# Both projections of a hybrid decoder layer as Strassen block products with seven instead of eight multiplications

## The chip, the cores and the metric

The kernel runs on one core of a Trainium2 chip. A core has TensorE (PE) for matmuls, whose results go to eight PSUM banks, VectorE (DVE), ScalarE (ACT) and GpSimd (POOL) for everything elementwise, and SyncE (SP), which here only issues DMAs. The metric is the time of one execution on the device, in microseconds (us); less is better. GpSimd has no access to PSUM.

## The reference

A sequence of 2048 tokens with 1024 channels is normalised, projected to 6144 columns, mixed by two groups of heads, normalised per head, gated, projected back, added to the input and normalised again. All in float32.

```python
xn = rms_norm(h, ln_g)                          # (2048, 1024)
proj = xn @ w_in                                # w_in (1024, 6144)
b_gate, c_gate, x_conv, g_conv, x_lru, g_lru = split(proj)      # six times 1024
y_conv = b_gate * conv3(c_gate * x_conv)                        # causal, per channel
y_conv = headwise_rms_norm(y_conv, 8, conv_out_g) * silu(g_conv)
u = conv4(x_lru) + lru_conv_b
r, i = sigmoid(u_head @ w_a + b_a), sigmoid(u_head @ w_i + b_i)  # 16 heads of 64
a = exp(8 * r * log_sigmoid(lam))
h_t = a_t * h_{t-1} + sqrt(1 - a_t**2) * (i_t * u_t)             # scan over tokens
y_lru = headwise_rms_norm(h_t, 16, lru_out_g) * silu(g_lru)
out = rms_norm(x + concat(y_conv, y_lru) @ w_out, final_g)      # w_out (2048, 1024)
```

## The kernel before

Channels lie on the partitions, 128 at a time, and tokens run along the free dimension. To keep float32 accuracy with the faster matmul format, every operand is split into a high part (rounded to that format) and a low part (the rest), and every product is three matmuls: high x high, high x low, low x high. A matmul here has a 128x128 stationary operand and a moving one of 128x512.

*Input projection.* The tokens are cut into four chunks of C = 512 (NC = 4). The normalised, transposed input of each chunk, xh[c] and xl[c], stays in SBUF. `load_w` (L215) loads one column tile of w_in (128 columns, all 1024 input channels), and GpSimd makes its two parts (L220, L221). `unit` (L224) multiplies one such tile with one chunk: 8 k tiles x 3 matmuls into one PSUM bank. The outer loop (L491) runs over steps of column tiles: "a" makes C and X and the short convolution (`conv_a`), "b" makes B and the gate G and finishes the conv head (`conv_b`), "l" makes an LRU tile and its gate (`lru`); the inner loop runs over the four chunks. `lru` computes the width-4 convolution u (L382, L385), stacks high and low halves of its two heads in stA and stB (L389, L390), and `lru_gates` multiplies them with the small gate matrices (L410). `lru_scan` does Tanh, Exp, Sqrt and the scan for two chunks at a time. `finish` (L265) applies gain and gate, spills the result to DRAM (yd) and prepares the squares whose sums over channels a matmul with a selector makes (L305); `head_norms` spills the reciprocal roots (rsd). `later` and `tick` put off matmuls that need such results by a few half steps.

*Output projection.* w_out is split and kept whole in SBUF (woh, wol). For each of 16 token blocks of 128, `load_z` (L459) loads the spilled rows and the head norms, multiplies them and splits; `out_mm` (L518) makes 2 x 16 x 3 matmuls into two banks; `epilogue` (L545) adds x, normalises and stores.

The tile framework schedules every engine's order by priority and readiness and inserts the semaphores.

Of the kernel before, what the change touches and what calls it, by code (L numbers as in the profile page):

```python
# [24 lines left out]
EPS = 1e-6  # L25

# columns of the packed per-channel parameters, eight per parameter row;
# b_i has its two heads swapped in each tile
# [3 lines left out]
# column groups of w_in, in tiles of 128  # L32
# [4 lines left out]
def hymba_kernel(ctx: ExitStack, tc: tile.TileContext, x, xt, w_in, par, lamc, w_gate, w_out, final_g, out):  # L37
# [3 lines left out]
    big = ctx.enter_context(tc.tile_pool(name="big", bufs=4))  # L41
    rawp = ctx.enter_context(tc.tile_pool(name="rawp", bufs=4))
    small = ctx.enter_context(tc.tile_pool(name="small", bufs=4))
    psu = ctx.enter_context(tc.tile_pool(name="psu", bufs=4, space=bass.MemoryType.PSUM))
    pss = ctx.enter_context(tc.tile_pool(name="pss", bufs=3, space=bass.MemoryType.PSUM))
# [4 lines left out]
    rsd = [dram.tile([NB, 3 * KT, P], F32, name=f"rsd{c}") for c in range(NC)]  # L50

    x0 = big.tile([P, NB, D], F32, tag="xl", name="x0")
    for b in range(NB):
        nc.sync.dma_start(x0[:, b, :], x[b * P:(b + 1) * P, :])
# [9 lines left out]
    # column P holds ones, columns 2P and 2P + KT ones for one 64-wide head each;  # L64
    # a sliding window puts them at any output row
    sel = const.tile([P, 3 * P], F32R, name="sel")
    nc.gpsimd.memset(sel.bitcast(F32), 0.0)
    nc.gpsimd.memset(sel.bitcast(F32)[:, P:P + 1], 1.0)
    nc.gpsimd.memset(sel.bitcast(F32)[:64, 2 * P:2 * P + 1], 1.0)
    nc.gpsimd.memset(sel.bitcast(F32)[64:, 2 * P + KT:2 * P + KT + 1], 1.0)  # L70
    ones = const.tile([P, P], F32R, name="ones")
    nc.gpsimd.memset(ones.bitcast(F32), 1.0)

    # 0 on the partitions of a head's high sums, -1 on those of the low ones
    lomask = const.tile([P, 1], F32, name="lomask")
    nc.vector.memset(lomask, 0.0)
    for p0 in (32, 96):
        nc.vector.memset(lomask[p0:p0 + 32, :], -1.0)

    # per-row divisor of the head sums: row 32c + j is head j of chunk c  # L80
    inv_hd = const.tile([P, 1], F32, name="inv_hd")
    nc.vector.memset(inv_hd, 1.0 / 64)
    for c in range(NC):
        nc.vector.memset(inv_hd[32 * c:32 * c + KT, :], 1.0 / 128)

    # klam = 8 * log_sigmoid(lam) = -8 * (relu(-lam) + log1p(exp(-|lam|)))
# [3 lines left out]
    def make_klam():  # L90
        lam = work.tile([P, 2, C], F32, tag="r", bufs=1, name="lam")[:, 0, 0:KT]
        nc.sync.dma_start(lam, lamc)
        w = [small.tile([P, KT], F32, tag=f"kl{j}", bufs=1, name="kl") for j in range(4)]
# [22 lines left out]
    xh = [None] * NC  # L116
    xl = [None] * NC
    norm_ps = psn.tile([P, C], F32, name="norm_ps")
    norm_first = [True]

    wp = ctx.enter_context(tc.tile_pool(name="wp", bufs=3))
    p1 = tc.tile_pool(name="p1", bufs=2)
    work = p1.__enter__()

    def wt(tag, name, bufs=2, dt=F32, n=C):
        return work.tile([P, n], dt, tag=tag, bufs=bufs, name=name)

# [5 lines left out]
    def alloc_xn(c):  # L133
        xh[c] = big.tile([P, KT, C], F32R, tag="xh", name=f"xh{c}")
        xl[c] = big.tile([P, KT, C], F32R, tag="xl", name=f"xl{c}")

    def prep_first():
        junk = big.tile([P, NB, D], F32, tag="xh", name="junk")
        for b in range(NB):
            ss = small.tile([P, 1], F32, tag="ss", name="ss")  # L140
            rs = small.tile([P, 1], F32, tag="rs", name="rs")
            nc.scalar.activation(out=junk[:, b, :], in_=x0[:, b, :], func=AF.Square, accum_out=ss)
            rstd(rs, ss)
            nc.vector.tensor_scalar(out=x0[:, b, :], in0=x0[:, b, :], scalar1=rs, scalar2=0.0,
                                    op0=ALU.mult, op1=ALU.add)
        alloc_xn(0)
        for k in range(KT):
            pool, tag = ((pss, "s"), (psu, "u"))[k % 2]
            tp = pool.tile([P, C], F32, tag=tag, name="tp")
            for b in range(NB):  # L150
                nc.tensor.transpose(tp[:, b * P:(b + 1) * P], x0[:, b, k * P:(k + 1) * P], ident)
            g = pt[:, LN_G + k:LN_G + k + 1]
            nc.scalar.activation(out=xh[0][:, k, :], in_=tp, func=AF.Copy, scale=g)
            nc.vector.scalar_tensor_tensor(out=xl[0][:, k, :], in0=tp, scalar=g,
                                           in1=xh[0][:, k, :].bitcast(F32),
                                           op0=ALU.mult, op1=ALU.subtract)
# [3 lines left out]
    def load_rows(c):  # L160
        rows = []
        early = big.tile([P, NB, D], F32, tag="xl", name="early") if c == 1 else None
        for b in range(NB):
            if c == 1:
                t = early[:, b, :]
            else:
                t = rawp.tile([P, D], F32, tag="raw", name="xrow")
            r0 = c * C + b * P
            nc.sync.dma_start(t, x[r0:r0 + P, :])
            rows.append(t)  # L170
        return rows

    def load_cols(c):
        cols = []
        cols4 = [work.tile([P, 2, C], F32, tag=tag, bufs=1, name="xcol2") for tag in ("r", "a", "T")]
        for k in range(KT):
            t = cols4[k // 2][:, k % 2, :] if k < 6 else wt("i", "xcol")
            nc.sync.dma_start(t, xt[k * P:(k + 1) * P, c * C:(c + 1) * C])
            cols.append(t)
        return cols  # L180

    def prep_sums(rows):
        ss = small.tile([P, NB], F32, tag="ss4", bufs=2, name="ss4")
        rs = small.tile([P, NB], F32, tag="rs4", bufs=2, name="rs4")
        for b in range(NB):
            nc.scalar.activation(out=rows[b], in_=rows[b], func=AF.Square, accum_out=ss[:, b:b + 1])
        rstd(rs, ss)
        rsh = small.tile([P, NB], F32R, tag="rsh", bufs=2, name="rsh")
        nc.vector.tensor_scalar(out=rsh, in0=rs, scalar1=1.0, scalar2=0.0, op0=ALU.mult, op1=ALU.add)
        nc.vector.tensor_tensor(out=rs, in0=rs, in1=rsh.bitcast(F32), op=ALU.subtract)  # L190
        dgh = wt("uh", "dgh", dt=F32R)
        dgl = wt("ul", "dgl", dt=F32R)
        for dg, part, eng in ((dgh, rsh.bitcast(F32), nc.vector), (dgl, rs, nc.gpsimd)):
            for b in range(NB):
                eng.tensor_scalar(out=dg[:, b * P:(b + 1) * P], in0=ident,
                                  scalar1=part[:, b:b + 1], scalar2=0.0,
                                  op0=ALU.mult, op1=ALU.add)
        return dgh, dgl

    def prep_chunk(c, dgs, cols):  # L200
        rb = pss.tile([P, C], F32, tag="s", name="rb")
        for n in range(2):
            nc.tensor.matmul(rb, ones, dgs[n], start=(n == 0), stop=(n == 1))
        alloc_xn(c)
        for k in range(KT):
            nc.vector.scalar_tensor_tensor(out=cols[k], in0=cols[k],
                                           scalar=pt[:, LN_G + k:LN_G + k + 1], in1=rb,
                                           op0=ALU.mult, op1=ALU.mult)
            nc.scalar.copy(xh[c][:, k, :], cols[k])
            eng = nc.gpsimd if k % 2 else nc.vector  # L210
            eng.tensor_tensor(out=xl[c][:, k, :], in0=cols[k],
                              in1=xh[c][:, k, :].bitcast(F32), op=ALU.subtract)

# [1 line left out]
    def load_w(j):  # L215
        raw = rawp.tile([P, D], F32, tag="raw", name="wraw")
        nc.sync.dma_start(raw, w_in[j])
        wh = wp.tile([P, D], F32R, tag="wh", name="wh")
        wl = wp.tile([P, D], F32R, tag="wl", name="wl")
        nc.gpsimd.tensor_scalar(out=wh, in0=raw, scalar1=1.0, scalar2=0.0, op0=ALU.mult, op1=ALU.add)  # L220
        nc.gpsimd.tensor_tensor(out=wl, in0=raw, in1=wh.bitcast(F32), op=ALU.subtract)  # L221
        return wh, wl
# [27 lines left out]
    def later(halves, f):  # L250
        queue.append([halves, f])
# [374 lines left out]
```

## Time and profile before

| | |
|---|---|
| time, median of 3 runs | 1579.53 us (1577.23 to 1580.32) |
| span of the profiled execution, first to last instruction | 1576.4 us |
| mean granted TensorE clock | 0.983 |
| matmuls | 6374 |
| busy: TensorE, VectorE, ScalarE, GpSimd | 96%, 49%, 35%, 23% |
| moved by DMA | 126.63 MB |

The profiled execution has no time of its own beside its span; the three runs are other executions of the same kernel. In the rows of the profile, a group of instructions is named by its line, engine, operation, written and read tiles, shapes and count; after the bar stand busy time (us), mean of one (ns) and the engine's idle time just before. A row of a window gives, after the length, the busy time and count of TensorE, its weight loads, VectorE, ScalarE and GpSimd, then the granted clock as a share, the busy share of the DMA engines and GB/s. In a timeline a row begins with start and duration in us.

### The profile page before, as it was taken

What the parts mean: (1) busy time and instruction counts of PE and PEld (TensorE: products, weight loads), DVE (VectorE), ACT (ScalarE), POOL (GpSimd) and SP (SyncE); (2) the same over time, 40 slices, a digit from 0 to 9 for tenths busy, and PEclk for the clock granted to TensorE, in tenths of its full rate; (3) what the DMA queues carried; (4) which work ended last, traced back from release to release, by engine and by line L of the source; (5) the groups of instructions that cost most, each with busy time, mean ns of one, the idle gap of its engine ahead of it and who ended that gap; (6) DMA issues with size and microseconds to landing.
All of it is one profiled execution on the core that took longest, in us unless ns stands there. A gap on an engine that the chain in (4) does not pass through costs nothing.

```text
span 1576.4 us, 16303 instructions
## 1 busy us (share of the span) xinstructions
PE 1510.8 (96%) x6374; PEld 1209.5 (77%) x6374; DVE 773.7 (49%) x927; ACT 558.0 (35%) x845; POOL 363.0 (23%) x267
## 2 busy tenths in 40 slices
PE   7999889998999899999989998999899999999998
PEld 6788677886888688778868886888687788888886
DVE  5765875257335633752464247325648533332331
ACT  6525554245226322542262236215336311111111
POOL 5531333203320322222232113320333100000000
PEclk9999999999999999999999999999999999999999
DMA  8420221012210211111121111110226754434420
GB/s 307 168 81 14 66 58 51 29 32 58 58 49 14 71 34 47 35 49 41 41 58 40 34 34 54 54 40 15 77 59 191 240 187 147 159 117 138 147 94 27
DMA packets 71289, 126.63 MB, mean 80 GB/s; under 512 B 7084, under 2 KB 41260, under 8 KB 71212
## 3 DMA queue, kind: packets, MB, share of 16 engines
q1 hardware_dynamic: 70924, 125.27, 25.4%
q8 instruction: 50, 0.82, 0.2%
q10 hardware_dynamic: 288, 0.32, 0.1%
q14 instruction: 27, 0.22, 0.0%
HBM read 91.81 MB, written 25.36 MB: 74 GB/s over the span
## 4 chain that ended last, share of the span: by engine, by line
PE 79%; DVE 9%; ACT 8%; issue 3%; DMA 1%; POOL 0%; SPq 0%; DVEq 0%; ACTq 0%; POOLq 0%
PE unit L232 54%; PE acc L524 22%; DVE u L433 2%; PE gate L410 2%; DVE u L385 1%; DVE a L435 1%; PE norm_ps L305 1%; ACT i L412 1%; ACT r L412 1%; DVE sg L266 1%; ACT L313 1%; ACT L427 1%; DVE u L414 1%; ACT stA L389 1%; DVE u L382 1%
## 5 line engine op out<-in xcount | busy, mean ns | idle before, releaser
L232 PE MATMUL unit<-xh,wh 128*128 128x512 f32 x1536 | 612.6, 399 | 0.0
L232 PE MATMUL unit<-xl,wh 128*128 128x512 f32 x1536 | 612.4, 399 | 0.0
L232 PE MATMUL unit<-xh,wl 128*128 128x512 f32 x1536 | 611.4, 398 | 0.0
L232 PEld LDWEIGHTS unit<-xh,wh 128*128 128x128 f32 x1536 | 292.0, 190 | 71.4
L232 PEld LDWEIGHTS unit<-xl,wh 128*128 128x128 f32 x1536 | 291.7, 190 | 71.2
L232 PEld LDWEIGHTS unit<-xh,wl 128*128 128x128 f32 x1536 | 291.5, 190 | 71.4
L524 PE MATMUL acc<-woh,zl 128*128 128x512 f32 x512 | 203.2, 397 | 2.2 <-DVE zl L473 2.2
L524 PE MATMUL acc<-woh,zh 128*128 128x512 f32 x512 | 203.0, 396 | 0.0
L524 PE MATMUL acc<-wol,zh 128*128 128x512 f32 x512 | 203.0, 396 | 0.0
L221 POOL TENSOR_TENSOR wl<-wraw,wh 128x1024 fp32r<-128x1024 f32 x48 | 120.2, 2504 | 3.8
L524 PEld LDWEIGHTS acc<-woh,zl 128*128 128x128 f32 x512 | 96.4, 188 | 26.5 <-DVE zl L473 3.1
L524 PEld LDWEIGHTS acc<-wol,zh 128*128 128x128 f32 x512 | 96.4, 188 | 23.5
L524 PEld LDWEIGHTS acc<-woh,zh 128*128 128x128 f32 x512 | 96.4, 188 | 23.4
L385 DVE SCALAR_TENSOR_TENSOR u<-xs,pt,u 128x512 f32<-128x512 f32 x96 | 96.3, 1003 | 2.7
L220 POOL TENSOR_SCALAR wh<-wraw 128x1024 fp32r<-128x1024 f32 x48 | 56.9, 1185 | 133.2 <-PE unit L232 125.6
L277 POOL TENSOR_TENSOR q<-q,q 64x512 f32<-64x512 f32 x32 | 42.7, 1335 | 170.0 <-ACT q L276 170.0
L473 DVE TENSOR_TENSOR zl<-zz,zh 128x1024 fp32r<-128x1024 f32 x32 | 41.8, 1305 | 76.2 <-ACT zh L472 76.2
L275 ACT ACTIVATE q<-t 64x512 f32<-64x512 f32 x32 | 20.2, 632 | 158.8 <-DVE t L352 149.7
L553 ACT ACTIVATE ob<-xr 128x512 f32<-128x512 f32 x32 | 20.1, 629 | 157.5 <-DVE xr L552 157.5
L472 ACT CAST zh<-zz 128x1024 fp32r<-128x1024 f32 x32 | 33.5, 1048 | 117.2 <-PE acc L524 108.6
L287 POOL TENSOR_TENSOR a<-a 128x512 f32<-128x512 f32 x32 | 41.0, 1301 | 146.9 <-DVE sg L266 142.5
L314 DVE TENSOR_TENSOR sg<-unit,sg 128x512 f32<-128x512 f32 x64 | 44.1, 689 | 60.6 <-ACT sg L313 60.6
(130 smaller groups left out, 1355.2 us busy)
## 6 DMA issues: line engine op xcount, KB each, us to landing
wraw<-in_w_in_dram SPq DMA_DIRECT2D x48, 512.0 KB, 3.5
yd<-sg SPq DMA_DIRECT2D x64, 256.0 KB, 2.3
zz<-yd SPq DMA_DIRECT2D x32, 512.0 KB, 4.1
qs<-a SPq DMA_DIRECT2D x128, 64.0 KB, 2.0
woraw<-in_w_out_dram SPq DMA_DIRECT2D x16, 512.0 KB, 3.8
zr<-rsd SPq DMA_DIRECT2D x32, 256.0 KB, 4.0
zr<-rsd SPq DMA_DIRECT2D x16, 512.0 KB, 5.9
xr<-in_x_dram SPq DMA_DIRECT2D x16, 512.0 KB, 5.8
```

Source lines behind the costliest of these rows:

```text
L220: nc.gpsimd.tensor_scalar(out=wh, in0=raw, scalar1=1.0, scalar2=0.0, op0=ALU.mult, op1=ALU.add)
L221: nc.gpsimd.tensor_tensor(out=wl, in0=raw, in1=wh.bitcast(F32), op=ALU.subtract)
L232: nc.tensor.matmul(ps, lhs, rhs, start=(n == 0), stop=(n == 3 * KT - 1))
L277: nc.gpsimd.tensor_tensor(out=q[lo], in0=q[lo], in1=q2[lo], op=ALU.add)
L287: nc.gpsimd.tensor_tensor(out=y, in0=y, in1=y, op=ALU.mult)
L314: nc.vector.tensor_tensor(out=sg, in0=gps, in1=sg, op=ALU.mult)
L385: nc.vector.scalar_tensor_tensor(out=u, in0=xs[:, j:j + C], scalar=lw[j], in1=u, op0=ALU.mult, op1=ALU.add)
L410: nc.tensor.matmul(ps, gw[n][:, j, :], st[j], start=(n == 0), stop=(n == 1))
L412: nc.scalar.activation(out=g[hi], in_=ps[src], func=AF.Sigmoid, bias=pt[src, bias + k:bias + k + 1])
L472: nc.scalar.copy(zh, zz)
L473: nc.vector.tensor_tensor(out=zl, in0=zz, in1=zh.bitcast(F32), op=ALU.subtract)
L524: nc.tensor.matmul(ps, lhs[:, k % KT, :], rhs[q][:, j, ds_], start=(k == KT and i == 0), stop=(k == KT - 1 and i == 2))
```

## The change

Every projection step becomes a 2x2 block product, [c11 c12; c21 c22] = A B, in the form of Strassen's scheme with seven multiplications and shared sums (Winograd's variant). A is the stationary side, B the moving one.

- *Input steps.* A step takes two column tiles (an "l", "a" or "b" pair, as before), so A's blocks are two tiles x two halves of the 1024 input channels, and B's are two channel halves x two chunks of 512 tokens. There are two passes over all 24 steps, one for each 1024 tokens (`h`); w_in is read in both. Of each block combination, `s_groups` makes the weight sums on VectorE and splits them (ScalarE the high parts; VectorE or GpSimd the low ones). `t_groups` does the same for the 7 x 4 moving tiles, which stay in SBUF for a whole pass.
- *Output steps.* The contraction over 2048 channels is cut into two passes (`ph`), first the LRU channels, then the conv ones. A step takes two token blocks as A and a set of w_out tiles as B. The first pass stores x plus its partial result to DRAM (od), the second adds it and normalises.
- A product is 4 k tiles x 3 matmuls, so a step has 84 matmuls instead of 96. Three products are accumulated on top of a bank that VectorE or ScalarE has read before; the other sums of products are made by VectorE from PSUM.
- TensorE's order is written out by hand (`tc.manual_schedule(engines={PE})`). A step has seven slots of one product. Slot by slot the weights of the next step are prepared, `load_next` loads two steps ahead, and elementwise work waits in `fifo`, from which each slot takes three items (`pop`). `later(n, f)` puts matmuls off by n slots. The first step after a change of B (steps 0, 24, 48, 56) runs over the k tiles on the outside instead, with seven banks open, while B's next tiles are being split.
- Elementwise work on a channel tile now takes 1024 tokens in one instruction; the conv and LRU states pass from the first half to the second through hx, hp and hl. Head sums take a high and a low part of the squares, two matmuls each for two chunks; the swaps of head halves by DMA are gone. The second half's normalised x^T is made during the first half (`second_sums`, `second_cols`) and stored in DRAM.

```diff
+    def s_groups(r, dst):                       # A: a11 a12 / a21 a22
+        a11, a12, a21, a22 = r
...
+        def g1():
+            t[1], t[2] = tmp(), tmp()
+            tt(t[1], a21, a22, ALU.add)
+            tt(t[2], t[1], a11, ALU.subtract)
+            sp2(1, t[2])                        # sp2: ACT copies the high part, eng subtracts
+        def g3():
+            tt(a21, a11, a21, ALU.subtract)
+            sp2(3, a21)
+        def g5():
+            tt(t[2], a12, t[2], ALU.subtract)
+            sp2(5, t[2])
+        return [lambda: sp2(0, a11, nc.gpsimd), g1, lambda: sp2(2, t[1]), g3,
+                lambda: sp2(4, a12, nc.gpsimd), g5, lambda: sp2(6, a22, nc.gpsimd)]
...
+    def mm(bank, S_, T_, i, j, start, stop, more=False):
+        sh, sl = S_[i]
+        th, tl = T_[i, j]
+        js = slice(j * P, (j + 1) * P)
+        for n, (a, b) in enumerate(((sh, th), (sh, tl), (sl, th))):
+            nc.tensor.matmul(bank, a[:, js], b, start=start and n == 0, stop=stop and n == 2,
+                             skip_group_check=more)
...
+            for s in range(7):                  # an ordinary step
+                if s == 0:
+                    prep(n, 6)
+                elif n + 1 < len(steps):
+                    prep(n + 1, s - 1)
...
+                tick()
+                i = s if s < 4 else {4: 0, 5: 2, 6: 3}[s]
+                if s < 4:
+                    bk[s] = bank()
+                for j in range(NB):
+                    mm(bk[i], S_, T, s, j, s < 4 and j == 0, j == NB - 1, s > 3)
+                if s == 0:
+                    q1 = sm("q1")
+                    nc.scalar.copy(q1, bk[0])
+                elif s == 1:
+                    u2 = sm("u2")
+                    tt(u2, bk[1], q1, ALU.add)
+                elif s == 2:
+                    rr = sm("rr")
+                    tt(rr, bk[2], u2, ALU.add)
+                elif s == 3:
+                    put(22, bk[3], rr)
+                elif s == 4:
+                    put(11, bk[0], None)
+                elif s == 5:
+                    put(12, bk[2], u2)
+                else:
+                    put(21, bk[3], u2)
+                pop(3)
...
+    def lru(h, k):                              # "l": after put(12) the chain goes to fifo
...
+        def stack():
...
+            for j, (hi, lo) in enumerate(((LO, HI), (HI, LO))):
+                nc.scalar.copy(st[j][hi], u[hi])
+                tt(st[j][lo], u[hi], st[j][hi].bitcast(F32), ALU.subtract)
+            later(3, lambda: gates(0))
+            later(5, lambda: gates(1))
...
+        def put(which, bank, other):
+            dst = {11: o1[:, 4:4 + C], 12: o1[:, 4 + C:4 + N2], 21: g[:, 0:C], 22: g[:, C:N2]}[which]
+            combine(dst, bank, other)           # ACT copy, or DVE bank + other
+            if which == 12:
+                fifo.extend([c0] + [lambda j=j: cj(j) for j in (1, 2, 3)] + [keep, stack])
+            if which == 21:
+                silu(g)
...
+    def finish(h, kt, y, sil, q, gain, col, row):
+        def f1():                               # gain and gate on DVE, then two DMAs to yd
...
+        def f2():
+            nc.scalar.activation(out=q, in_=y, func=AF.Square)
+        def f3():                               # split of the squares
...
+            later(3, lambda: head_sums(h, qh, ql, col, row))
+        fifo.extend([f1, f2, f3])
...
+        def s0(): # u = i*u on DVE, Tanh;  s1: Exp;  s2: Square;  s3: (q+1)*T on DVE
...
+        # s4: Sqrt;  s5: T*u on DVE;  s6: scan, then finish
...
+    psu = ctx.enter_context(tc.tile_pool(name="psu", bufs=5, space=bass.MemoryType.PSUM))
+    pss = ctx.enter_context(tc.tile_pool(name="pss", bufs=2, space=bass.MemoryType.PSUM))
```

The comments in the diff that begin with "#" are this document's. In `conv_a`, m0 multiplies the two products and two taps follow (m1 on ScalarE, mj on VectorE); in `conv_b`, `put(11)` and `put(12)` multiply into the conv result.

More of the change, by code (lines that the diff above doesn't have):

```diff
@@ L114, in make_klam, with later @@
         nc.vector.tensor_scalar(out=klam, in0=acc, scalar1=-8.0, scalar2=None, op0=ALU.mult)
[L116 to L126, printed above, removed]
+    fifo = []
+    due = []
+    def later(slots, f):
+        due.append([slots, f])
@@ new lines, in tick, with pop, tt, split @@
+    def tick():
+        for item in due:
+            item[0] -= 1
+        now = [item for item in due if item[0] <= 0]
+        due[:] = [item for item in due if item[0] > 0]
+        for item in now:
+            item[1]()
+    def pop(n):
+        n = max(n, -(-len(fifo) // 8))
+        for _ in range(min(n, len(fifo))):
+            fifo.pop(0)()
+    def tt(out, a, b, op, eng=None):
+        (eng or nc.vector).tensor_tensor(out=out, in0=a, in1=b, op=op)
+    def split(v, hi, lo, eng):
+        nc.scalar.copy(hi, v)
+        tt(lo, v, hi.bitcast(F32), ALU.subtract, eng)
@@ L182, in prep_sums @@
[L182 to L198, printed above, removed]
@@ L215, in load_w @@
[L215 to L222, printed above, removed]
-    def unit(w, c):
-        wh, wl = w
-        ps = psu.tile([P, C], F32, tag="u", name="unit")
-        n = 0
-        for k in range(KT):
-            ks = slice(k * P, (k + 1) * P)
-            for lhs, rhs in ((wh[:, ks], xh[c][:, k, :]), (wh[:, ks], xl[c][:, k, :]),
-                             (wl[:, ks], xh[c][:, k, :])):
-                nc.tensor.matmul(ps, lhs, rhs, start=(n == 0), stop=(n == 3 * KT - 1))
-                n += 1
-        return ps
@@ new lines, in second_sums, with one, last @@
+    def second_sums():
+        for c in range(2):
+            ss = small.tile([P, NB], F32, tag="ss4", bufs=2, name="ss4")
+            rs = small.tile([P, NB], F32, tag="rs4", bufs=2, name="rs4")
+            for b in range(NB):
+                def one(b=b, c=c, ss=ss):
+                    t = wt(("stA", "stB")[b % 2], "xrow")
+                    r0 = ((2 + c) * NB + b) * P
+                    nc.sync.dma_start(t, x[r0:r0 + P, :])
+                    nc.scalar.activation(out=t, in_=t, func=AF.Square, accum_out=ss[:, b:b + 1])
+                yield one
+            def last(c=c, ss=ss, rs=rs):
+                rstd(rs, ss)
+                nc.sync.dma_start(rsx[c].rearrange("b p -> p b"), rs)
+            yield last
@@ new lines, in gates @@
+        def gates(i):
+            sl = slice(i * C, (i + 1) * C)
+            if i == 0:
+                v["r"], v["i"] = wt("r", "r"), wt("ig", "i", bufs=IG)
+            ps = []
+            for j in range(2):
+                ps.append(pss.tile([P, C], F32, tag="s", name="gate"))
+                for n in range(2):
+                    nc.tensor.matmul(ps[j], v["gw"][n][:, j, :], v["st"][j][:, sl],
+                                     start=(n == 0), stop=(n == 1))
+            for j, (hi, lo) in enumerate(((LO, HI), (HI, LO))):
+                for g_, src, bias in ((v["r"], hi, BA), (v["i"], lo, BI)):
+                    nc.scalar.activation(out=g_[hi, sl], in_=ps[j][src], func=AF.Sigmoid,
+                                         bias=pt[src, bias + k:bias + k + 1])
+            if i == 1:
+                fifo.extend([s0, s1, s2, s3, s4, s5, s6])
@@ new lines, in put, with combine @@
+        def put(which, bank, other):
[5 more added lines that the diff above has]
+                silu(g)
+        return put
+    def combine(dst, bank, other):
+        if other is None:
+            nc.scalar.copy(dst, bank)
+        else:
+            tt(dst, bank, other, ALU.add)
@@ new lines, in conv_b, with put @@
+    def conv_b(h, k):
+        t = tcur["t"]
+        g = wt("o2", "gb", bufs=O2)
+        def put(which, bank, other):
+            if which == 11 and other is None:
+                tt(t[:, 0:C], bank, t[:, 0:C], ALU.mult)
+            elif which == 11 or which == 12:
+                b = small.tile([P, C], F32, tag="rr", name="bb")
+                combine(b, bank, other)
+                sl = slice(0, C) if which == 11 else slice(C, N2)
+                tt(t[:, sl], b, t[:, sl], ALU.mult)
+            else:
+                combine(g[:, 0:C] if which == 21 else g[:, C:N2], bank, other)
+            if which == 21:
+                silu(g)
+                finish(h, k, t, g, t, pt[:, CG + k:CG + k + 1], R, k)
+        return put
```

770 lines of the change are left out of this document (399 added, 371 removed).

## The prediction

> **What bounds the kernel now.** I read the page's first part for the busy engines, the table of windows for the matmul's pace in each stage, the waits of TensorE for what is not pace, and then the grouped rows of VectorE, GpSimd and ScalarE, because the change buys matmuls with additions on those three.
>
> ```profile
> span 1576.4 us, 16303 instructions
> PE 1510.8 (96%) x6374; PEld 1209.5 (77%) x6374; DVE 773.7 (49%) x927; ACT 558.0 (35%) x845; POOL 363.0 (23%) x267
> PE 79%; DVE 9%; ACT 8%; issue 3%; DMA 1%; POOL 0%; SPq 0%; DVEq 0%; ACTq 0%; POOLq 0%
> ```
>
> ```profile
> 0.00:57.00 57.00, 48.12 (x207) 38.25 (x208) 35.42 (x79) 37.79 (x74) 29.27 (x38) 1.00 0.82 289
> ...
> 332.00:480.00 148.00, 142.09 (x601) 113.88 (x601) 70.78 (x81) 54.13 (x79) 39.10 (x28) 0.98 0.15 44
> ...
> 1238.00:1570.00 332.00, 331.82 (x1417) 266.42 (x1415) 115.55 (x149) 55.17 (x106) 0.00 (x0) 1.00 0.41 135
> ```
>
> TensorE bounds it: 96% busy and 79% of the chain. The last window is the output projection, where nothing interrupts it: 331.82 us over 1417 matmuls is 0.2342 us for each matmul of 512 columns. The middle window is one channel tile of the input projection: 601 x 0.2342 = 140.8 of its 148 us, so 7.2 us are lost. The waits say on what:
>
> ```profile
> PE gate L410 <- DVE stA L390: 45.6, 9, 5.9
> ```
>
> ```profile
> 375.58 0.77 PE L410 MATMUL gate<-stA,bh 128*128 128x512 f32 x1 [5.91 <-DVE stA L390]
> 376.14 0.63 PE L410 MATMUL gate<-stA,bl 128*128 128x512 f32 x1
> 376.57 0.63 PE L410 MATMUL gate<-stB,bh 128*128 128x512 f32 x1
> ...
> 378.65 0.40 PE L232 MATMUL unit<-xh,wh 128*128 128x512 f32 x1
> 378.89 0.40 PE L232 MATMUL unit<-xl,wh 128*128 128x512 f32 x1
> ```
>
> The gate products of the LRU wait for VectorE, at the longest 5.91 us, and then matmuls start 0.43 us apart instead of 0.24 for some 3 us: seven or eight slow ones add about 1.5 us. All told the span holds 1576.4 - 6374 x 0.2342 = 83.6 us that are not matmul pace. VectorE is at half load.
>
> **What goes.** Each projection block of 96 matmuls becomes seven products of four k tiles and three split terms, 84. There are 48 input steps and 16 output steps, so 64 x 84 = 5376 against 6144. Gate products stay at 128, head sums go from 64 to 128 (a high and a low part, 512 tokens each). The broadcasts (6) go, transposes double to 64 and fall in the start. That is 5632 wide matmuls x 0.2342 = **1319 us**. A gate or head-sum matmul is counted like any other.
>
> **What comes, on VectorE.** One triple of input steps (l, a, b) holds 3 x 84 + 8 + 8 = 268 matmuls, 62.8 us of TensorE. Prices:
>
> ```profile
> L314 DVE TENSOR_TENSOR sg<-unit,sg 128x512 f32<-128x512 f32 x64 | 44.1, 689 | 60.6 <-ACT sg L313 60.6
> L428 DVE TENSOR_TENSOR r<-a 128x1024 f32<-128x1024 f32 x16 | 19.5, 1222 | 16.6 <-ACT a L427 16.6
> L429 DVE SCALAR_TENSOR_TENSOR T<-r,T 128x1024 f32<-128x1024 f32 x16 | 20.3, 1268 | 0.3
> L435 DVE TENSOR_TENSOR_SCAN a<-a,u 128x512 f32<-128x512 f32 x24 | 30.2, 1259 | 0.6
> L385 DVE SCALAR_TENSOR_TENSOR u<-xs,pt,u 128x512 f32<-128x512 f32 x96 | 96.3, 1003 | 2.7
> L266 DVE SCALAR_TENSOR_TENSOR sg<-t,pt,sg 128x512 f32<-128x512 f32 x32 | 37.1, 1159 | 1.1
> L266 DVE SCALAR_TENSOR_TENSOR sg<-a,pt,sg 128x512 f32<-128x512 f32 x32 | 22.7, 735 | 0.0
> ```
>
> Weight combinations and their splits: 8 per step, 24 x 0.69 = 16.6. Combining products: 5, 5 and 7, 17 x 0.69 = 11.7, of which 16 read PSUM (11.0). Wide multiply-adds (three LRU taps, two conv taps, s3, two gains): 8 x 1.27 = 10.2. Wide additions and products (s0, s5, m0, two stacks, two q splits): 7 x 1.22 = 8.5. One scan of 1024: 2.5. Sum **49.5 us**, 79% of the 62.8. In the first half of the tokens, 16 scalings of x^T add about 0.75 each, 1.5 us per triple.
>
> **GpSimd and ScalarE.**
>
> ```profile
> L221 POOL TENSOR_TENSOR wl<-wraw,wh 128x1024 fp32r<-128x1024 f32 x48 | 120.2, 2504 | 3.8
> L287 POOL TENSOR_TENSOR a<-a 128x512 f32<-128x512 f32 x32 | 41.0, 1301 | 146.9 <-DVE sg L266 142.5 <-ACT csb L321 4.4
> L369 POOL TENSOR_TENSOR bl<-bd,bh 128x256 fp32r<-128x256 f32 x8 | 6.6, 820 | 0.7
> ```
>
> ```profile
> L412 ACT ACTIVATE r<-gate,pt 64x512 f32<-64x512 f32 x64 | 43.7, 683 | 6.5 <-PE gate L410 5.5
> L427 ACT ACT_TABLE_LOAD x16 | 20.5, 1283 | 0.3
> L389 ACT CAST stB<-u 64x512 fp32r<-64x512 f32 x32 | 19.7, 617 | 3.1 <-DVE sq L293 2.4
> L427 ACT ACTIVATE a<-r,klam 128x1024 f32<-128x1024 f32 x16 | 18.4, 1153 | 0.2
> ```
>
> GpSimd per triple: 9 low parts x 1.30, two silu products x 2.50, one gate weight 0.82: 17.5 us. ScalarE: 26 narrow copies x 0.62, 8 gate sigmoids x 0.68, 14 wide ones x 1.15, some four table loads x 1.28: 42.8 us. Neither is near 62.8. They are not independent, though:
>
> ```profile
> 419.40 2.41 POOL L221 TENSOR_TENSOR wl<-wraw,wh 128x1024 fp32r<-128x1024 f32 x1
> 420.00 3.14 DVE L342 SCALAR_TENSOR_TENSOR t<-p,pt,t 128x512 f32<-128x512 f32 x2 [0.80 <-ACT t L340]
> ```
>
> ```profile
> 371.80 1.71 POOL L291 TENSOR_TENSOR a<-a,qs 128x512 f32<-128x512 f32 x1
> 372.31 0.68 DVE L314 TENSOR_TENSOR sg<-unit,sg 128x512 f32<-128x512 f32 x1
> ```
>
> Two VectorE operations that take about 0.74 each alone lasted 3.14 us: they ran out when GpSimd's product ended at 421.81. A product that reads PSUM (L314, 0.68) lost nothing beside GpSimd. The same instruction at L266 averages 1159 ns in one place and 735 in the other. So VectorE's cost per triple lies between 49.5 (GpSimd meets only gaps and PSUM readers) and 49.5 + 17.5 = 67.0 (every GpSimd product holds it up). L385 and L266 alone lost 96 x 0.27 + 32 x 0.42 = 39 us to it, against 363 us of GpSimd, with VectorE 49% busy; the other contended rows would bring that to perhaps a quarter. At 79% load I take 40%, 7 us: **56.5 us**, just inside TensorE's 62.8. This is the step I trust least.
>
> The Trainium skill, page "SBUF — State Buffer", section "Who interferes with whom", says that VectorE and GpSimd share a port pair under an exclusive lock: when a VectorE instruction has two SBUF inputs and GpSimd reads SBUF, the later one blocks until the other ends. The row of 3.14 us agrees, and so does the PSUM reader that lost nothing. Taken for every GpSimd product, that rule gives the 67.0 us and a projection bound by VectorE; the averages above give 56.5.
>
> **Stalls of TensorE in a triple.** TensorE follows a written order, so a late operand holds everything behind it. The first gate product stands two product slots into step a; it needs the LRU's u, finished only after the sixth product of step l. That chain: product 0.69 (combine), c0 on ScalarE 1.15, three taps 3 x 1.27, copy 1.15, two stack halves 2 x 1.22: 9.2 us. TensorE covers three slots of 12 matmuls, 8.4 us. VectorE also has about 2.8 us of other work queued there (one combination with its split, two combines), and one or two GpSimd products of 1.3. So between 0.8 and 6 us; I take 4, near the 5.91 that the old chain showed. Behind it in TensorE's queue stand products whose operands are ready. The second suspect is the LRU's head sum: from the second gate product, four sigmoids, Tanh, Exp, Square, Sqrt, two more wide ScalarE passes, two table loads, four wide VectorE operations and the scan come to about 4 x 0.68 + 6 x 1.15 + 2 x 1.28 + 4 x 1.25 + 2.5 = 19.7 us; seven slots and four matmuls cover 20.6. That margin is thin: 0 to 3, I take 1. Together **5 us per triple, 16 x 5 = 80**. Slow matmuls after a stall add up to 1.5 us where it is over some 3 us; that is inside the range.
>
> The Trainium skill, "TensorE: Matmul & The Clock Gate", Part 1, has the array at half clock after an idle window of about 3.4 us. The 0.43 us spacing after the 5.91 us wait agrees. By it, stalls of 4 us would each pay the 1.5 us, 24 us more than my sum; stalls below 3 us none.
>
> **Start.**
>
> ```profile
> 14.46 0.48 PE L232 MATMUL unit<-xh,wh 128*128 128x512 f32 x1
> ```
>
> Today the first 57 us hold 175 wide matmuls (207 less 32 transposes), 41 us, so 16 are lost. Afterwards both halves of a 1024-token set must be normalised, turned, combined and split before step 0 can end: per k tile 8 VectorE operations, 32 x 0.69 = 22 us, step 0's own 5.5, eight row scalings and the turns about 10, the lambda constants about 10, GpSimd's low parts 15 x 1.30 = 20 of which a third collides. From about 6 us on this is some 54 us, so step 0 ends near 60 with 19.7 us of matmuls in it: **40 lost** (from 16, as today, to 60).
>
> **Three changes of operand set** (second half of the tokens, two halves of the output contraction). Each splits 28 new moving tiles while 84 matmuls run: VectorE 32 x 0.69 = 22, plus half of GpSimd's 12 x 1.30, 30 us against 19.7. **11 each, 33 in all** (0 to 20 each: part may run during the step before).
>
> **Costed at nothing.** Input weights are read twice and the second half's x^T and a partial output make a round trip through memory.
>
> ```profile
> GB/s 307 168 81 14 66 58 51 29 32 58 58 49 14 71 34 47 35 49 41 41 58 40 34 34 54 54 40 15 77 59 191 240 187 147 159 117 138 147 94 27
> zr<-rsd SPq DMA_DIRECT2D x32, 256.0 KB, 4.0
> ```
>
> A triple moves some 4.2 MB, about 65 GB/s; an output step 4 MB in 19.7 us, about 200, below the 240 that one slice shows. Loads are issued about two steps, some 30 us, ahead of use, against 4 us to landing; a late one would stop VectorE's normalising product, then the weight combinations behind it. SyncE issues more, smaller DMAs; the 128 swaps of head halves go. In an output step VectorE has 17 x 0.69, 11.7 us, plus 2.5 in the second phase, against 19.7.
>
> **End.**
>
> ```profile
> 1569.43 0.39 PE L524 MATMUL acc<-woh,zl 128*128 128x512 f32 x1
> ...
> 1572.05 1.42 DVE L561 SCALAR_TENSOR_TENSOR ob<-xr,rs,fg 128x512 f32<-128x512 f32 x2
> 1573.50 0.35 ACTq L564 DMA_DIRECT2D out_dram<-ob  x1
> ```
>
> From the last matmul to the end are 6.6 us; a 1024-wide addition and square make it **8**.
>
> **Sum** against the profiled span of 1576.4: 1319 + 80 + 40 + 33 + 8 = 1480. The median of the runs, 1579.53, is 3.1 above that span: **1483 us**.
>
> **Rivals.** *Covered* (0.18): the schedule keeps VectorE's chains short; stalls of 1 us per triple, 5 per set change, 35 at the start: 1319 + 16 + 15 + 35 + 8 + 3 = 1396. For it: the idle half of VectorE today. Against: gate stalls already at that half load. *Half covered* (0.15): stalls of 8.5 to 10.5 us per triple, mostly on VectorE's backlog: 1540 to 1570. *VectorE and GpSimd bound* (0.12, slower): every GpSimd product holds VectorE, 67.0 us per triple, and waits on ScalarE between split and subtraction leave it 10 us idle: 77 per triple, 14.2 of stall, 1319 + 227 + 40 + 33 + 8 + 3 = 1630. It decides the sign from 62.8 + 11 = 73.8 us per triple on. For it: L266's 1159 ns. Against: PSUM readers, a quarter of VectorE's work, escape the lock.
>
> **How the numbers follow.** The forecast (0.52) spans 1425 to 1535, from stalls of 2 to 8 us per triple. A measurement of this kernel tells about 0.2% from no change; 0.03 goes to that band. Faster: 0.18 + 0.52 + 0.15 = 0.85; slower 0.12. The range 1395 to 1580 leaves out half of the covered case (0.08) and the bound one (0.12).
>
> **What the next profile would show.** About 5696 matmuls; pace still 0.234 in undisturbed windows, clock near 1.0; VectorE near 80% and GpSimd near 30% between 60 and 1130 us; TensorE's largest wait on the stacked halves, tens of us over 16 times; L385's successor above 1.27 us wherever GpSimd is busy; step 0 ending near 60. I am wrong if VectorE is over 90% busy there with TensorE waiting for weight splits or freed banks, if the gate wait is absent, or if the output steps wait for loads.

## The result and the profile after

1756.66 us (median, 1755.29 to 1758.92) against 1579.36 us: **1.1125 times** the time before (95% interval 1.1109 to 1.114). Slower, far above the predicted 1483 and its range. The page of the changed kernel, first its engines and the granted clock in 40 slices:

```profile
span 1753.2 us, 16673 instructions
PE 1450.5 (83%) x5696; PEld 1136.8 (65%) x5696; DVE 1288.5 (73%) x1434; ACT 827.8 (47%) x1211; POOL 573.7 (33%) x360
PEclk8888898899898998899899989899898899988999
```

TensorE has 678 instructions less and is busy 83% instead of 96%. VectorE is busier but not full. The waits of TensorE (engine and line, released by, us in total, times, longest):

```profile
PE gate L445 <- DVE stA L151: 65.0, 16, 6.6
PE norm_ps L349 <- ACT qh L370: 64.8, 30, 6.2
PE norm_ps L349 <- DVE ql L151: 49.9, 30, 3.4
PE tp L288 <- DVE x L279: 28.1, 8, 12.1
PE bank L601 <- ACT th L159: 23.6, 10, 4.8
PE bank L601 <- DVE tl L151: 20.5, 17, 3.6
PE bank L601 <- DVE rr L151: 20.2, 8, 6.4
PE gate L445 <- DVE stB L151: 6.5, 11, 1.0
```

The largest are not the products themselves: the gate products (65.0 + 6.5) and the head sums (64.8 + 49.9), small matmuls that stand in the written order ahead of ready work. One triple in the timeline, the same VectorE instruction in two consecutive ones, then TensorE at two of the three places:

```profile
821.83 0.69 DVE L151 TENSOR_TENSOR xl<-bank,u 128x512 f32<-128x512 f32 x1 [4.15 <-PE bank L601]
...
900.40 0.69 DVE L151 TENSOR_TENSOR xl<-bank,u 128x512 f32<-128x512 f32 x1 [4.15 <-PE bank L601]
```

```profile
829.34 0.39 PE L601 MATMUL bank<-tl,sh 128*128 128x512 f32 x1
829.57 0.39 PE L601 MATMUL bank<-th,sl 128*128 128x512 f32 x1
833.26 0.47 PE L445 MATMUL gate<-stA,bh 128*128 128x512 f32 x1 [3.31 <-DVE stA L151]
...
861.90 0.39 PE L601 MATMUL bank<-th,sl 128*128 128x512 f32 x1
863.63 0.44 PE L349 MATMUL norm_ps<-qh,sel 128*64 128x512 f32 x1 [1.34 <-ACT qh L370]
866.75 0.69 PE L349 MATMUL norm_ps<-ql,sel 128*64 128x512 f32 x1 [2.69 <-DVE ql L151]
867.24 0.63 PE L349 MATMUL norm_ps<-qh,sel 128*64 128x512 f32 x1
867.67 0.63 PE L349 MATMUL norm_ps<-ql,sel 128*64 128x512 f32 x1
868.09 0.63 PE L601 MATMUL bank<-th,sh 128*128 128x512 f32 x1
...
871.93 0.63 PE L601 MATMUL bank<-th,sh 128*128 128x512 f32 x1
```

A triple takes 78.6 us. Undisturbed products start 0.227 us apart (829.34 to 829.57), so its 268 matmuls need 60.8; **17.8 us** are lost. In this triple the waits at the three places are 10.4 us of it (over all 16 triples they average 186.2 / 16 = 11.6); the other 7.4 are matmuls that start up to 0.43 us apart after a wait (868.09 to 871.93). The third place, in the same triple, shows that two short waits with one matmul between them are enough for that:

```profile
888.44 0.44 PE L349 MATMUL norm_ps<-qh,sel 128*64 128x512 f32 x1 [1.72 <-ACT qh L370]
889.70 0.69 PE L349 MATMUL norm_ps<-ql,sel 128*64 128x512 f32 x1 [0.82 <-DVE ql L151]
890.19 0.63 PE L349 MATMUL norm_ps<-qh,sel 128*64 128x512 f32 x1
890.61 0.63 PE L349 MATMUL norm_ps<-ql,sel 128*64 128x512 f32 x1
```

The two long stretches of the input projection lose about as much, 17.7 us per 268 matmuls in the second half of the tokens and 20.7 in the first:

```profile
80.00:700.00 620.00, 519.78 (x2039) 407.75 (x2038) 434.56 (x469) 320.96 (x442) 168.85 (x121) 0.90 0.25 76
...
770.00:1290.00 520.00, 450.24 (x1777) 354.18 (x1777) 360.85 (x383) 261.60 (x351) 136.06 (x86) 0.91 0.20 57
```

VectorE over one triple:

```profile
827.00:906.00 79.00, 68.58 (x272) 54.02 (x271) 54.57 (x58) 39.66 (x54) 21.29 (x14) 0.91 0.19 56
```

It is busy 54.6 of 79 us. It does not bound this stage; its results come too late for TensorE's order. Why late is partly GpSimd, as here, where two taps of the LRU's convolution take 5.08 us instead of 2 x 1.28:

```profile
823.90 1.28 DVE L420 SCALAR_TENSOR_TENSOR u<-xl,pt,u 128x1024 f32<-128x1024 f32 x1
825.70 5.08 DVE L420 SCALAR_TENSOR_TENSOR u<-xl,pt,u 128x1024 f32<-128x1024 f32 x2
826.96 2.74 POOL L151 TENSOR_TENSOR gl<-gl,sg 128x1024 f32<-128x1024 f32 x1 [0.59 <-ACT sg L381]
```

Below, one of the four executions of the kernel with gates at 5 and 7 slots took 2252.04 us at a granted clock of 0.557; it is left out of that kernel's ratio, and the other three took 1538 to 1542 us.

### The profile page after: what moved, and what is told of

The parts are those of the page before. It is cut to its first block, busy times and chain, and to the rows that moved or that the text cites. A ratio compares the mean times of both kernels' runs of the same rounds, so it can differ in the third digit from the quotient of the medians.

```text
span 1753.2 us, 16673 instructions
## 1 busy us (share of the span) xinstructions
PE 1450.5 (83%) x5696; PEld 1136.8 (65%) x5696; DVE 1288.5 (73%) x1434; ACT 827.8 (47%) x1211; POOL 573.7 (33%) x360
## 5 line engine op out<-in xcount | busy, mean ns | idle before, releaser
L601 PE MATMUL bank<-th,sh 128*128 128x512 f32 x1792 | 745.6, 416 | 58.7 <-ACT th L159 23.6
L601 PE MATMUL bank<-tl,sh 128*128 128x512 f32 x1792 | 739.4, 413 | 20.5 <-DVE tl L151 20.5
L601 PE MATMUL bank<-th,sl 128*128 128x512 f32 x1792 | 732.1, 409 | 0.0
L151 POOL TENSOR_TENSOR sl<-raw,sh 128x512 fp32r<-128x512 f32 x192 | 300.4, 1565 | 889.3 <-ACT sh L159 852.9
L601 PEld LDWEIGHTS bank<-th,sh 128*128 128x128 f32 x1792 | 362.4, 202 | 155.5 <-ACT th L159 29.2
L601 PEld LDWEIGHTS bank<-tl,sh 128*128 128x128 f32 x1792 | 362.9, 202 | 106.9 <-DVE tl L151 27.6
L601 PEld LDWEIGHTS bank<-th,sl 128*128 128x128 f32 x1792 | 361.0, 201 | 79.9
L159 ACT CAST sh<-raw 128x512 fp32r<-128x512 f32 x256 | 157.7, 619 | 339.4 <-PE bank L601 226.6
L159 ACT CAST sh<-st 128x512 fp32r<-128x512 f32 x192 | 117.2, 619 | 221.4 <-PE bank L601 145.1
L151 DVE TENSOR_TENSOR sl<-st,sh 128x512 fp32r<-128x512 f32 x192 | 157.3, 823 | 4.1 <-ACT sh L159 3.8
L151 DVE TENSOR_TENSOR raw<-raw,zr 128x512 f32<-128x512 f32 x64 | 73.4, 1156 | 44.3 <-DMA zr<-rsd 38.9
L349 PE MATMUL norm_ps<-qh,sel 128*64 128x512 f32 x64 | 35.0, 547 | 64.8 <-ACT qh L370 64.8
L349 PE MATMUL norm_ps<-ql,sel 128*64 128x512 f32 x64 | 40.1, 626 | 49.9 <-DVE ql L151 49.9
```

The source lines that it names most:

```text
L151: (eng or nc.vector).tensor_tensor(out=out, in0=a, in1=b, op=op)
L159: nc.scalar.copy(hi, v)
L349: nc.tensor.matmul(norm_ps[0], sel[:, s0:s0 + R], q[:, i * C:(i + 1) * C], start=norm_ps[1] == 0, stop=norm_ps[1] == 8 * KT - 1)
L601: nc.tensor.matmul(bank, a[:, js], b, start=start and n == 0, stop=stop and n == 2, skip_group_check=more)
```

## The experiments

The theory (A): gates and head sums are placed too early in TensorE's order, and slow matmuls follow each wait. The rival (B): VectorE together with GpSimd is the bound, and a wait removed comes back elsewhere.

**Later slots.**

```diff
-            later(3, lambda: head_sums(h, qh, ql, col, row))
+            later(5, lambda: head_sums(h, qh, ql, col, row))
-            later(3, lambda: gates(0))
-            later(5, lambda: gates(1))
+            later(4, lambda: gates(0))
+            later(6, lambda: gates(1))
```

> The gate products are put off by one more product slot (4 and 6 slots instead of 3 and 5), the head sums by two more (5 instead of 3); nothing else changes. Theory A (TensorE stands in its written order before operands that come some 4 us late at three places of each triple of input steps, and runs slow for 2 to 3 us after each): the gate wait falls from about 4.5 to 1.8 us, the two head-sum waits of 4 and 3.5 us nearly vanish, and most of the slow matmuls with them: 10 us of waits and 4 of slow pace less per triple, 16 x 14 = 220, so about 1530 us. Theory B (VectorE together with GpSimd is the bound, so a wait removed here comes back at another instruction): 1700 to 1755 us, with new waits of the projection's matmuls for weight splits or banks.

1574.15 us, 0.9968 of the kernel before (0.9958 to 0.9978): 182 less for three numbers. Theory B had at least 1700; theory A had 1530, and is missed by 44. Waits on the head sums fall from 114.7 to 13.0, on the gates from 71.5 to 49.7. In the second half of the tokens the projection runs nearly without loss, with VectorE at 162 of 200 us:

```profile
900.00:1100.00 200.00, 193.96 (x846) 156.33 (x845) 162.02 (x178) 119.29 (x166) 71.35 (x42) 1.00 0.24 71
```

**Order in finish.** `fifo.extend([f2, f3, f1])` for `[f1, f2, f3]`, and the conv squares get the idle tile "u".

> In finish, the squares and their split go ahead of the gain-and-gate product, and the conv squares get a tile of their own, so the head sums no longer stand behind the product that waits for GpSimd's silu. Gates as in the changed kernel. Theory A: the conv head sum's wait (about 3.5 us and 2 of slow pace) vanishes and the LRU's loses about 1.3 us: 16 x 6 to 7, about 1650 us. Theory B: 1740 to 1760.

1675.12 us, 1.0601 (1.0583 to 1.0619): 82 less, somewhat short of A. The head-sum waits halve, to 63.3.

**GpSimd does not read in the splits.** In `split`, where GpSimd would subtract:

```diff
+        if eng is not None:
+            nc.gpsimd.memset(lo.bitcast(F32), 0.0)
+            return
```

> GpSimd no longer makes low parts by subtraction: a memset that reads nothing writes zeros in their place (the low parts of products 0, 4 and 6 of the weights and 0, 4 and 5 of the moving side are left out of the computation; the matmuls still run). GpSimd's silu products and wide adds stay. Theory A: the chains in front of the three waits shorten by 1 to 3 us each, 16 x about 5 plus some slow pace: 1640 to 1690 us. Theory B: the lock on VectorE goes for 11.3 of 17.5 us per triple, so the whole input projection follows: below 1570.

1601.73 us, 1.0138 (1.0119 to 1.0156): 155 less, between the two theories and more than A gave. GpSimd's part is a second cause, not a detail. The waits at gates (54.7) and head sums (71.1) are still there. The edit does more than end the reading: a memset takes 0.53 us instead of 1.57 and need not wait for ScalarE's high part, so these 155 us are not all GpSimd's hold on VectorE.

**TensorE kept busy before the three places.** `warm_up()` runs 12 matmuls of the coming product into an unread bank, ahead of `gates(0)` and `head_sums`.

> Ahead of the first gate product and of each head sum, 12 matmuls of the coming product run into a bank that nobody reads, so TensorE is busy for 2.7 us of each wait; the operands' lateness is as before. 48 more matmuls per triple, 11 us at full pace. If the slow pace after a wait costs what the trace shows (8 to 11 matmuls at 0.43 instead of 0.23 us, three times a triple): about 16 x 5 = 80 us less, 1675 us. If the waits are no real waits (the operands come late because TensorE is late): 1755 + 130 to 180 us. If the clock plays no part: 1755.

1694.37 us, 1.072 (1.0694 to 1.0746): 62 less with 552 matmuls more. The expectation counted 48 such matmuls per triple; there are 36 at most (three times 12). The waits at the three places fall from 186.2 to 70.2 us, 116 less, and the extra matmuls take 552 x 0.2267 = 125, so the gain is one of pace: the granted clock is 0.953 on average instead of 0.902. Here idle TensorE before a late operand is worse than useless work.

**Later slots and order together.**

> The later slots of the first experiment together with the order of finish of the second (squares and split ahead of the gain product). If both only remove the same head-sum waits, this takes away the 13 us of head-sum waits that the first still shows and a little of slow pace, 1550 to 1565 us; if the order also relieves VectorE's queue in front of the gates, 1530 to 1550; 1575 or more if VectorE is the bound by now.

1562.8 us, 0.9884 (0.9851 to 0.9916): they remove mostly the same waits.

**Later slots and no reading by GpSimd.**

> The later slots and no reading by GpSimd in the splits (the same low parts left out as in the third experiment). Alone they gave 182 and 155 us less than the changed kernel. If both remove the same thing, the lateness of operands at the three places, together they give little more than the better one: 1490 to 1560, with the gain where the first experiment still waits (gates 50 us, set changes). If VectorE's blocked time is a bound of its own beside them: near the sum, 1420 to 1460.

1456.5 us, 0.9221 (0.9202 to 0.9241): 300 less than the changed kernel, near the sum 182 + 155, some 37 shared. This has the low parts left out.

**Other tiles for the norms in the output steps.** `piece("zr")` becomes one of the tiles "u", "r", "stA", "stB" from step 51 on.

> The later slots, and in the output steps from the fourth on the head norms are loaded into four tiles that stand empty there instead of into the ten shared small ones, so that the loads need not wait for a tile. If the output steps lose their time because these loads are issued late (VectorE's normalising product stands first in its queue and waits, 39 us in the changed kernel): 20 to 40 us less than the 1574 of the later slots alone. If they lose it to VectorE's load and GpSimd's hold on it: within 5 us of 1574.

1575.17 us, 0.9965 (0.9949 to 0.998), as without it. VectorE's waits for these norms fell from 42.2 to 26.7 us and the time did not follow, so this lateness is not what the output steps lose.

**Gates two slots later**, at 5 and 7, with head sums at 5 and the new order in finish.

> As the previous combination of later slots and order, but with the gate products at 5 and 7 slots instead of 4 and 6. If what is left at the gates (44 us in the first experiment) is still lateness: 30 to 50 us less than that combination. If the later gates push the LRU's own chain to its head sum, 5 us per triple come back there: within 20 us of it.

1540.74 us, 0.9747 (0.9729 to 0.9766): 22 less than with 4 and 6, less than lateness promised but no loss. Gate waits are down from 45.2 to 10.7 us in all; some of that comes back at products that wait for VectorE's rr (34.3 to 44.8 us), as the rival B would have it. Two triples and more now hold 608 matmuls in 140 us; what remains lies in the start, the set changes and the output steps:

```profile
425.00:565.00 140.00, 138.64 (x608) 112.54 (x607) 120.05 (x130) 88.05 (x121) 52.14 (x35) 1.00 0.23 69
565.00:700.00 135.00, 109.18 (x437) 84.94 (x435) 124.09 (x126) 83.48 (x119) 57.24 (x34) 0.89 0.29 84
...
1220.00:1330.00 110.00, 101.19 (x433) 81.62 (x432) 87.43 (x92) 31.41 (x55) 57.91 (x30) 0.98 0.69 207
```

**The output steps without GpSimd.** `s_groups` takes its engine for low parts from the step's kind, and `fin` adds on VectorE.

> On top of the best combination so far (gates at 5 and 7 slots, head sums at 5, squares ahead of the gain product; 1541 us): in the output steps all of GpSimd's work goes to VectorE (three low parts and two wide additions per step). VectorE executes 3 x 0.69 + 2 x 1.22 = 4.5 us more per step, and GpSimd's 3 x 1.6 + 2 x 2.9 = 10.6 us no longer hold it. If the hold is what the output steps lose (they run at 25 us instead of 19): 16 x 3 to 5, 1460 to 1500 us. If they lose it to late loads: 1535 to 1545. If VectorE's own work binds: 1560 or more.

1493.83 us, 0.9469 (0.9446 to 0.9491): 47 less, within what the hold said. VectorE executes more instructions and the window of output steps is full:

```profile
1180.00:1260.00 80.00, 79.45 (x350) 65.17 (x349) 73.45 (x107) 23.79 (x40) 0.00 (x0) 1.00 0.84 251
```

**All low parts on VectorE.**

```diff
-        return [lambda: sp2(0, r[0], nc.gpsimd), g1, lambda: sp2(2, t[1]), g3,
-                lambda: sp2(4, r[2], nc.gpsimd), lambda: sp2(5, r[3], nc.gpsimd), g6]
+        return [lambda: sp2(0, r[0]), g1, lambda: sp2(2, t[1]), g3,
+                lambda: sp2(4, r[2]), lambda: sp2(5, r[3]), g6]
```

and the same in `s_groups` for every step.

> As the kernel before it in this set, but every low part of the whole kernel is made by VectorE, in the input projection and in the set changes too; GpSimd keeps the silu products and the gate weights. Nothing is left out of the computation. VectorE executes 9 x 0.69 = 6.2 us more per triple and is held 11.7 us less. If the hold was a real part of VectorE's time: the set changes and the start shorten by 5 to 8 us each, the triples stay at 62 us: 1440 to 1480. If VectorE's executed work is what counts (49.5 + 6.2 of 61 us per triple): stalls return, 1520 or more.

**1449.34 us, 0.9177 (0.9152 to 0.9201)**, 8.2% faster than the kernel before and with nothing left out.

```profile
PE 1328.3 (92%) x5696; PEld 1072.1 (74%) x5696; DVE 1271.8 (88%) x1704; ACT 821.4 (57%) x1211; POOL 119.4 (8%) x90
```

```profile
565.00:640.00 75.00, 53.46 (x204) 40.75 (x205) 70.68 (x98) 41.07 (x62) 8.08 (x4) 0.84 0.37 105
...
700.00:840.00 140.00, 140.00 (x618) 114.61 (x617) 128.97 (x153) 89.01 (x122) 13.65 (x8) 1.00 0.25 71
```

VectorE made 270 instructions more than in the changed kernel in 17 us less busy time (1271.8 against 1288.5): waiting for GpSimd had counted as busy. From 700 to 840 us TensorE is busy all the time. At the first set change (565 to 640 us) 75 - 204 x 0.2267 = 29 us are lost, with VectorE at 94%.

**The same engines with the old slots and order.**

> The changed kernel's own slots and order, with all low parts and the wide output additions on VectorE as in the best kernel (1449 us). So it differs from that one by lateness alone, and from the changed kernel (1757) by GpSimd's hold alone. If the two causes are separate and add up: the late slots and the order gave 216 us with GpSimd's hold in place (1757 to 1541); the same here gives 1665. If they share a part, since operands are late partly because VectorE is held: less is left to gain from the slots, 1560 to 1630. If the hold were the whole cause: below 1480.

1644.61 us, 1.0415 (1.0387 to 1.0444). That is 20 less than separate causes gave and 15 more than the upper end of shared ones. So the two causes stand in a square, GpSimd's low parts and wide additions left there or moved to VectorE, against early or late: 1757 and 1541 with GpSimd, 1645 and 1449 without. Lateness (slots and order) costs 216 and 195, GpSimd 112 and 91; each is nearly the same whichever way the other stands, and some 20 us are shared.

This kernel also prices the hold. It has the slots and order of the changed kernel, and by the means of its own rows the 270 added VectorE instructions take 200 us (240 low parts at 0.683, 30 additions at 1.217); VectorE is busy 1273.2 us in all. So in the changed kernel some 1288.5 - (1273.2 - 200) = 215 us of VectorE's busy time were waiting for GpSimd, an estimate. No run separates this hold from GpSimd's own slowness (1.57 us for a low part); for the hold speaks that among TensorE's waits in the changed kernel none is for a GpSimd instruction.

**Layout.** High and low part as halves of one tile.

> The changed kernel with high and low parts of each split as two halves of one tile instead of two tiles. The matmuls of the changed kernel start 0.227 us apart when undisturbed, those of the kernel before 0.234. If the place of the operands in memory sets this, the pace moves here, towards 0.234; if not, it stays 0.227 and the time 1755 us.

1760.45 us in a single run; products still start 0.227 us apart (11.56 us for 51 steps):

```profile
899.76 11.95 PE L601 MATMUL bank<-th,sh 128*128 128x512 f32 x52
```

## Why the prediction was wrong

*What goes, and its price.* 5696 matmuls, as counted. The pace was mis-sized the other way: 0.2267 instead of 0.2342 us, 5632 x 0.0075 = 42 us in the change's favour. The seven products do save what they promise.

*Stalls of TensorE in a triple* is the step that failed: 5 us taken, 17.8 measured; with this triple for all sixteen, 16 x 12.8 = 205 us of the 273 between the summed span of 1480 and 1753. The whole account, with 0.2267 us for each matmul taken off: the start loses 59 us, the two long stretches of triples 158 and 117, the three stretches around a set change (700 to 770, 1290 to 1410, 1530 to 1620 us) 31, 40 and 27, the other output steps and the end 43. That is 475 where the sum had 161, less the 42 of the pace. The parts of the triple's loss: the gate wait was 4.5 (71.5 / 16) where I took 4, from the right chain. The two head sums took 114.7 / 16 = 7.2 where I took 1 for the LRU's and nothing for the conv head's. That chain was never costed: `finish` puts its gain product first, which waits for GpSimd's silu, and the squares queue behind. The waits that show it on VectorE:

```profile
DVE gb L359 <- POOL gb L151: 53.5, 12, 9.2
```

And the slow pace, 7.4 us in the triple shown, was left "inside the range" though I had quoted the rows that price it; three waits per triple pay it three times. Nor does it need one wait of over 3 us, as I had assumed: 1.72 and 0.82 us were enough. The clock rule of the Trainium skill ("TensorE: Matmul & The Clock Gate", Part 1) would have added 24 us to my sum. Even then it would have fallen short, because it was applied to one wait per triple, and to none below 3 us. That the pace is a part of its own shows in the kernel that keeps TensorE busy before the three places: 62 us back with more matmuls.

*VectorE's cost* was near: 54.6 us per triple where I had 56.5, and 49.5 + 6.2 = 55.7 with all low parts, where the windows show (128.97 / 140 of a 60.8 us triple) 56.0. But I compared it with TensorE's total and concluded that it was covered. GpSimd's work cost 91 to 112 us, in the changed kernel without VectorE being full in the triples: a hold lengthens each chain. The rule of the Trainium skill's page "SBUF — State Buffer" (section "Who interferes with whom") fits the 5.08 us. It also fits the mean of VectorE's low parts: in the changed kernel, with GpSimd's memset that reads nothing, and with GpSimd out of the splits they took 823, 712 and 682 ns:

```profile
L151 DVE TENSOR_TENSOR sl<-st,sh 128x512 fp32r<-128x512 f32 x192 | 157.3, 823 | 4.1 <-ACT sh L159 3.8
```

```profile
L151 DVE TENSOR_TENSOR sl<-st,sh 128x512 fp32r<-128x512 f32 x192 | 136.0, 712 | 2.6 <-ACT sh L159 2.4
```

```profile
L151 DVE TENSOR_TENSOR sl<-st,sh 128x512 fp32r<-128x512 f32 x192 | 129.7, 682 | 3.2 <-ACT sh L159 3.0
```

Even the best kernel still pays some of it. GpSimd's silu product still meets the last of the LRU's three taps there, so that the taps average 1948 ns against the 1.28 us of an undisturbed one:

```profile
L420 DVE SCALAR_TENSOR_TENSOR u<-xl,pt,u 128x1024 f32<-128x1024 f32 x48 | 93.5, 1948 | 0.8
```

*Start:* I had 40 lost, step 0 ending near 60; it ended near 78. At 80 us there were 94 wide matmuls (158 less 64 transposes), 21 us of work: 59 lost. The turns (transposes) wait 28.1 us for rows that VectorE normalises, 17.4 of it for the second 512 tokens (longest 12.1), and the granted clock is 0.81.

```profile
0.00:80.00 80.00, 41.43 (x158) 31.74 (x159) 59.98 (x105) 42.93 (x78) 27.88 (x28) 0.81 0.29 103
```

*Set changes:* 11 each predicted (30 less 19.7 is in fact 10); the clean reading in the best kernel is 29 for the first. I had counted the splits and left out that VectorE still carries the step before: it is at 94% there, though no run takes that load away to show it.

*Costed at nothing:* the loads of the head norms were rightly covered (the other tiles changed nothing). The output steps were not: in the changed kernel they ran 459 x 0.2267 = 104 in 120 us even between the set changes.

```profile
1420.00:1480.00 60.00, 50.55 (x214) 40.89 (x213) 46.23 (x49) 13.53 (x23) 27.82 (x15) 0.94 0.68 207
1480.00:1540.00 60.00, 57.66 (x245) 46.90 (x245) 43.62 (x50) 16.50 (x28) 31.21 (x16) 0.97 0.58 189
```

*The rivals.* "VectorE and GpSimd bound" gave the right side and 1630 us, but by a mechanism that three changed slot numbers refute: the later slots took 182 us away while GpSimd worked as before. GpSimd's work is a real cause beside them, but cost 91 to 112 us where this rival had 227 us of stalls. "Covered" had the right picture of a triple, only not for this placing: with later slots and GpSimd out of the way the whole kernel stands at 1449, under my own sum.

*The signs.* Between 60 and 1130 us VectorE was 71% busy and GpSimd 28%, and the largest wait was on the stacked halves, as forecast. Of the three signs of being wrong only the last came, VectorE's 38.9 us of waits for the head norms in the output steps, and the other tiles showed that these were not what cost the time. No sign looked for a second and third late operand. What did give them away was the clock: 0.89 there, where I had expected it near 1.0.

## What to carry to other kernels

When an engine's order is written by hand, cost every small dependent matmul by its own chain, from the last product it needs to its slot, and put it where the slowest chain ends: here one to two slots too few, in three places, together with the order in `finish`, cost some 200 us, more than the 710 wide matmuls saved were worth (166 us at 0.234). A wait of the matmul engine is priced with the slow matmuls behind it. And GpSimd work on SBUF beside a two-input VectorE stream was not free help here: moving it onto a VectorE that was 84% busy (the kernel with gates at 5 and 7 slots) made that engine's busy time smaller, 1271.8 us instead of 1293.0.

## What the runs showed of the hardware

The same matmul (128x128 stationary, 128x512 moving) ran at 0.2342 us for 1417 in a row before, and at 0.2267 in undisturbed products of the changed kernel. Its second gate products, which wait for nothing, start 0.23 to 0.24 apart:

```profile
842.12 0.40 PE L445 MATMUL gate<-stA,bh 128*128 128x512 f32 x1
842.36 0.39 PE L445 MATMUL gate<-stA,bl 128*128 128x512 f32 x1
842.59 0.40 PE L445 MATMUL gate<-stB,bh 128*128 128x512 f32 x1
```

Putting high and low parts into one tile did not move it. Whether the written order of TensorE, the place of its operands or something else makes the difference of 3% stays open; no run here separates them.
